# Three PE convolution tiles instead of six, stored weight parts in layer two, and a last stage in two parts per row

## The chip, the cores and the metric

One core of a Trainium2 chip runs the whole program. It has four compute engines, each with its own instruction stream taken strictly in order: PE (TensorE, matrix multiplies), DVE (VectorE), ACT (ScalarE) and POOL (GpSimd). A fifth stream, SP, issues every DMA of this kernel. The metric is device time in microseconds (us) for one execution. [...]

## The reference

A sequence of 2048 tokens of 1024 channels goes through two layers and a final RMSNorm. Layer one mixes a causal pooling and a state-space scan; the change leaves it alone. Layer two is the part that matters here:

```
h    = rmsnorm(x)
val, gt, z = split(h @ w_in, 3)                       # w_in: 1024 x 3072
g    = val * sigmoid(gt)
c    = depthwise_causal_conv(g, conv_w) + conv_b      # 31 taps for each of 1024 channels
c    = layernorm_over_channels(c) * ln_g + ln_b
x    = x + (silu(c) * silu(z)) @ w_out                # w_out: 1024 x 1024
out  = x * rsqrt(mean(x*x) + eps) * final_norm
```

All inputs and outputs are float32.

## The kernel before

**Halves and units.** The tokens are processed in two halves, A and B, of 1024. PE's work is a fixed list of units: layer one's projections of A and of B, its output of A, layer two's projections of A, layer one's output of B, layer two's projections of B, and then the last projection of A (`A.q`) and of B (`B.q`). A projection unit makes one tile of 128 channels by 1024 tokens with 48 matmuls of 128x512, since each product of float32 numbers is taken in three (high by high, high by low, low by high) of parts in fp32r. An output unit is 48 matmuls as well. Layer two of a half has 24 projection units: `g` and `v` for each channel tile j (gate and value), then eight `y` units (the second gate z).

**Weights.** A weight tile is loaded into `raw`; ACT rounds it into a high part (`w<-raw`, a CAST) and DVE subtracts for the low part. Four pairs of `w` slots exist; `fetch_thread` loads, `split_thread` splits. Half B loads and splits the same weights again.

**Convolution.** Each channel tile of a half is convolved by DVE or by PE. On DVE, ACT makes the first tap into an accumulator `ca`, and 30 SCALAR_TENSOR_TENSOR instructions add one tap each to the same accumulator. The last two tiles are done in two token blocks of 512. On PE (`pe_conv`) the tile goes through DRAM buffers `gpd`, a band of the taps is spread by ACT with a mask (24 instructions for each of two channel halves), and each channel half takes two chunks of 12 matmuls. `PEB = (6, 7)` are tiles that PE convolves for both halves at once; `PEC` adds 4 and 5 for half B alone. So PE convolves six of the sixteen half-tiles in four passes, and DVE the other ten.

**Layer norm and gates.** `ln_thread(h, b, ...)` normalises one block b of 512 tokens of half h, when all eight channel tiles of that half are stored in `cd`. It loads four tiles, sums them (DVE), gets the mean from PE, subtracts, squares (ACT), gets the variance from PE, takes a power on POOL, spreads it by PE, and multiplies. PE thus holds three small groups of matmuls for each of the four blocks, at fixed places of its stream. Half A's results go through DRAM (`y1d`) and are split by `y1_thread`; `A.q` needs block 0, then block 1. `B.q` needs those of half B.

**Last stage.** `evac1` takes a row tile of 128 tokens: the residual is loaded, the matmul's result added for each channel half eh, ACT sums the squares, and with the second half POOL makes the factor `rs` and DVE scales 1024 columns by `rs` and `final_norm` in one instruction; one DMA stores them.

**What sets the order.** All this is written as generators. When the program is built, a planner (`Sched`) steps them with estimated durations and emits, engine by engine, the instruction that can start first, ties broken by RANK; PE's unit list has the lowest rank and fills what is left. So the streams' order depends on the estimates, but is fixed in the program. `Alloc` takes slots of a pool (`ca` 2, `cg` 2, `w` 8); `free` gives them back.

Of the kernel before, what the change touches and what calls it, by code (L numbers as in the profile page):

```python
# [10 lines left out]
F32 = mybir.dt.float32  # L11
F32R = mybir.dt.float32r
# [25 lines left out]
PAD = {("PE", True): 5.0, ("PE", False): 0.3, ("V", True): 1.0, ("V", False): 0.05, ("A", True): 1.0, ("A", False): 0.05}  # L38
SLOTS = dict(act=25, w=8, raw=2, st=8, po=2)
NSSM = 3  # L40
RANK = dict(split=2, pool=4, pec=3, lna=8, lnb=3, y1=3, ssm=4, prep=2)
PEB = (6, 7)
PEC = (4, 5) + PEB
ORDER = (range(NK), (0, 1, 6, 7, 2, 3, 4, 5))


VECS = {"even_norm": 8, "odd_norm": 8, "pool_scale": 4, "ssm_d": 4, "conv_b": 8, "conv_ln_g": 8, "conv_ln_b": 8}
# [29 lines left out]
class Sched:  # L77
# [170 lines left out]
def trunk(ctx, tc, io):  # L248
# [13 lines left out]
    def slots(pool, n, width=1024, where=const):  # L262
        sc.pool(pool, n, lambda i, dt, name: where.tile([128, width], dt, tag=f"{pool}{i}", name=name))
# [4 lines left out]
    slots("st", SLOTS["st"], SLOT)  # L268
    slots("po", SLOTS["po"], SLOT)
    slots("cg", 2, SLOT)  # L270
    slots("ca", 2)
    slots("sml", 12, 16)
    slots("pwt", 1, 128)
    slots("sml2", 1, 64)
# [17 lines left out]
    def width(o):  # L292
        return int(np.prod(o.shape[1:]))
# [94 lines left out]
    def mmb(batch):  # L388

        d = 0.0  # L390
        for o, w, x, s, e in batch:
            if x.dtype == F32R:
                d += width(o) / 2216.0
            elif w.shape[1] > 64:
                d += max(0.224, width(o) * 1e-3)
            else:
                d += 0.07 + width(o) * 0.5e-3

        def emit():
            for o, w, x, s, e in batch:  # L400
                nc.tensor.matmul(o, w, x, start=s, stop=e)  # L401
        rd = []
        wr = []
        for o, w, x, s, e in batch:
            for l, ap in ((rd, w), (rd, x), (wr, o)):
                if not any(ap is y for y in l):
                    l.append(ap)
        op = Op("PE", d, rd, wr, emit)
        op.n = len(batch)
        return op  # L410
# [68 lines left out]
    class Job:  # L479
        def __init__(self, src, name, key=("go",)):  # L480
            self.src, self.name, self.pool, self.key = src, name, "w", key

        def release(self):
            free(self.pool, self.hi, self.lo)

    def job_cols(w, c0, name):
        return Job(w[c0 // 128], name)
# [10 lines left out]
    jobs = []  # L498
    jobs_parts = {}

    def fetch_thread(jobs):
        for job in jobs:
            job.raw = yield Alloc("raw")
            yield Wait(job.key)
            yield dma(job.raw, job.src)
            done("raw", job)

    def split_thread(jobs):
        for job in jobs:
# [918 lines left out]
    def conv_load():  # L1428
        for h, j in conv_order:
            yield Wait(("g", h, j))  # L1430
            gt = yield Alloc("cg")
            if h == 0:
                yield gset(gt[:, :HL], 0.0)
            else:
                yield dma(gt[:, :HL], gd[0][j][:, H - HL:H])
            yield dma(gt[:, HL:HL + H], gd[h][j])
            cgt[h, j] = gt
            yield Wait(("cw",))
            ca = cas[h, j] = yield Alloc("ca")
            yield act(ca[:, :H], gt[:, 0:H], AF.Identity, bias=vc("conv_b", j), scale=cwt[:, j, 0:1])  # L1440
            done("cg", h, j)

    cgt, cas = {}, {}

    def conv_thread():

        seq = [(h, j, (0, 1)) for h, j in conv_order[:-2]]
        seq += [(h, j, (b,)) for b in range(2) for h, j in conv_order[-2:]]
        for h, j, bl in seq:
            yield Wait(("cg", h, j))  # L1450
            gt, ca = cgt[h, j], cas[h, j]
            n0, n1 = bl[0] * 512, bl[-1] * 512 + 512
            acc = ca[:, n0:n1]
            for k in range(1, NT):
                yield stt(acc, gt[:, k + n0:k + n1], cwt[:, j, k:k + 1], acc, ALU.mult, ALU.add)
            if bl[-1] == 1:
                free("cg", gt)
            spawn(conv_store(h, j, ca, bl), 6, f"cs{h}{j}")

    def conv_store(h, j, ca, bl):  # L1460
# [124 lines left out]
    def ln_thread(h, b, out, gate=None):  # L1585
        if gate:
            yield Wait(gate)
        bs = slice(b * 512, (b + 1) * 512)
        for j in range(NK):
            yield Wait(("c", h, j, b))  # L1590
        if h == 0 or b == 0:
            ct = yield Alloc("act", 4)
            pools = ("act",) * 4
        else:
            pools = ("ca", "ca", "cg", "cg")
            ct = yield Alloc("ca", 2)
            ct += yield Alloc("cg", 2)
        cc = [c[:, :1024] for c in ct]
        for kp in range(4):
            yield dma(k2(cc[kp]), cd[h][kp][:, :, bs])  # L1600
        sm_, vs_, q_ = yield Alloc("st", 3)
        sm, vs, sq = sm_[:, :1024], vs_[:, :1024], q_[:, :1024]
        yield tt(sm, cc[0], cc[1], ALU.add)
        for c in cc[2:]:
            yield tt(sm, sm, c, ALU.add)
        yield tt(sm[:, 0:512], sm[:, 0:512], sm[:, 512:1024], ALU.add)
        mups = yield Alloc("aux")
        yield mmb([(mups, onesN, sm[:, 0:512], True, True)])
# [85 lines left out]
    def evac1(h):  # L1694
        tag = f"{P[h]}.q"

        def half(eh, tp, s, ps):
# [3 lines left out]
            if eh == 0:  # L1701
                yield dma(xt[:, 0:512], rowd[:, 0:512])
            else:
                yield dma(xt[:, 512:1024], rowd[:, 512:1024])
                yield Wait(("x2", h, t))
                yield dma(xt[:, 0:512], x2d[h][t])
            yield Wait(("pe", tag, eh, tp, s))
            xv = xt[:, eh * 512:(eh + 1) * 512]
            yield tt(xv, xv, ps[:, s * 512:(s + 1) * 512], ALU.add)
# [9 lines left out]
            yield tt(ms, ssq[h][:, t, 0:1], ssq[h][:, t, 1:2], ALU.add, G)  # L1719
            yield ts(ms, ms, 1.0 / D, RMS_EPS, ALU.mult, ALU.add, G)  # L1720
            yield from rsqrt_of(rs, ms, 1)
            yield Wait(("fnb", h))
            x = xt[:, :1024]
            yield stt(x, x, rs, fnb[0], ALU.mult, ALU.mult)
            free("sml", sm)
            r0 = h * H + t * 128
            yield dma(io["out"][0, r0:r0 + 128, :], x)
            free("st", xt)

        def f(eh, tp, ps):  # L1730
# [120 lines left out]
    spawn(after(("y1d", 0, 3), ln_thread(0, 1, None)), RANK["lna"], "lnA1")  # L1851
    spawn(y1_thread(0, y1[0], ("u", GATE_Y)), RANK["y1"], "y1A0")
    spawn(after((y1[0].name, 7, 0), y1_thread(1, y1[0], ("u", GATE_Y))), RANK["y1"], "y1A1")
    spawn(ln_thread(1, 0, y1[1]), RANK["lnb"], "lnB0")
    spawn(ln_thread(1, 1, y1[1]), RANK["lnb"], "lnB1")
    spawn(fnb_thread(0, ("u", "A.q.e0t3")), 4, "fnb")
    done("fnb", 1)
    sc.run()
# [42 lines left out]
```

## Time and profile before

| what | us |
|---|---|
| median of 3 runs (1501.55 to 1502.56) | 1502.55 |
| the profiled execution | 1500.32 |
| its span, first to last instruction | 1498.5 |
| PE busy | 1467.7 |
| DVE busy | 1104.4 |
| ACT busy | 524.7 |
| DMA queue's packets, share of 16 engines | 55.5% |

In the profile a row of the timeline gives start, duration, engine, line, operation, output<-inputs with buffer numbers left out, shape and count, and in brackets the idle time just ahead of it with what ended it. A row of the wait list says which line waited for which engine, the total, the number of times and the longest. Lines L319, L337, L351, L363 and L401 are the helpers that record a tensor_tensor, a scalar_tensor_tensor, an ACT copy, an ACT activation and a matmul, so groups are told apart by tile names.

In time, layer two of half A begins on PE at 576 us, layer one's output of B follows from 847 us, layer two of half B from 983 us, `A.q` from 1303 us and `B.q` from about 1398 us.

### The profile page before, as it was taken

How to read it: one execution, taken by the hardware profiler on the slowest of the kernel's cores; microseconds unless marked ns; L12 is line 12 of the kernel's file. 1: busy time of each engine (PE TensorE's matmuls, PEld its weight loads, DVE VectorE, ACT ScalarE, POOL GpSimd, SP SyncE). 2: the span in 40 equal slices, each digit the busy share in tenths (PEclk: the TensorE clock that was granted, in tenths of full speed). 3: DMA queues.
4: the chain of work that ended last, by engine and by line, in shares of the span. 5: the costliest groups of instructions: out<-in, count | busy, mean ns of one | idle time of the engine just before them, and what ended most of it. 6: DMA issues, size and time to landing. Idle time of an engine off the chain costs nothing. (4 is left out here: it accounts for less than half of the span.)

```text
span 1498.5 us, 17919 instructions
## 1 busy us (share of the span) xinstructions
PE 1467.7 (98%) x6768; PEld 1202.1 (80%) x6768; DVE 1104.4 (74%) x1333; ACT 524.7 (35%) x834; POOL 89.7 (6%) x297
## 2 busy tenths in 40 slices
PE   7999899999999999999999999999999999999997
PEld 5887688888888888888888888888888788887785
DVE  7988583997975224699999998247987998987632
ACT  6235341112143035211111521352364556544411
POOL 1000100000000011000000000110000000003321
PEclk9999999999999999999999999999999999999999
DMA  9579946556475462331343543524557475957752
GB/s 350 197 212 335 336 165 247 194 189 239 161 268 151 125 206 85 112 111 59 99 127 113 210 140 128 183 70 128 109 156 227 138 244 185 385 202 248 260 171 109
DMA packets 161159, 276.26 MB, mean 184 GB/s; under 512 B 53184, under 2 KB 83632, under 8 KB 161072
## 3 DMA queue, kind: packets, MB, share of 16 engines
q1 hardware_dynamic: 161072, 275.12, 55.5%
q8 instruction: 53, 0.87, 0.2%
q14 instruction: 34, 0.28, 0.1%
HBM read 181.56 MB, written 93.51 MB: 184 GB/s over the span
## 5 line engine op out<-in xcount | busy, mean ns | idle before, releaser
L401 PE MATMUL mm<-act,w 128*128 128x512 f32 x4224 | 1003.8, 397 | 9.6 <-ACT act L363 6.6
L401 PEld LDWEIGHTS mm<-act,w 128*128 128x128 f32 x4224 | 793.2, 189 | 190.5 <-ACT act L363 6.6
L337 DVE SCALAR_TENSOR_TENSOR ca<-cg,cwt,ca 128x1024 f32<-128x1024 f32 (+1 forms) x360 | 397.5, 1106 | 12.8 <-ACT ca L363 2.5
L401 PE MATMUL mm<-w,act 128*128 128x512 f32 x1344 | 315.9, 395 | 0.8 <-DVE w L319 0.8
L401 PEld LDWEIGHTS mm<-w,act 128*128 128x128 f32 x1344 | 251.7, 188 | 59.4 <-DVE w L319 1.1
L319 DVE TENSOR_TENSOR w<-raw,w 128x1024 fp32r<-128x1024 f32 (+1 forms) x119 | 141.9, 1195 | 106.8 <-ACT w L351 106.1
L351 ACT CAST w<-raw 128x1024 fp32r<-128x1024 f32 (+1 forms) x119 | 121.6, 1022 | 214.9 <-PE mm L401 141.6
L363 ACT ACTIVATE junk<-st 128x1024 bf16<-128x1024 f32 (+1 forms) x64 | 54.0, 844 | 123.8 <-DVE st L319 116.1
L319 DVE TENSOR_TENSOR st<-st,mm 128x512 f32<-128x512 f32 x48 | 30.9, 683 | 76.2 <-PE mm L401 76.2
L351 ACT CAST act<-st 128x512 fp32r<-128x512 f32 (+1 forms) x64 | 51.8, 855 | 57.2 <-DVE st L337 16.6
L363 ACT ACTIVATE po<-mm 128x1024 f32<-128x1024 f32 x28 | 28.7, 1025 | 112.4 <-PE mm L401 70.7
L319 DVE TENSOR_TENSOR act<-st,act 128x512 fp32r<-128x512 f32 (+1 forms) x64 | 56.4, 922 | 14.7 <-ACT act L351 14.6
L401 PE MATMUL aux<-st,act 128*128 128x128 f32 (+2 forms) x448 | 63.8, 289 | 0.0
L363 ACT ACTIVATE act<-act,mask 128x128 f32<-128x128 f32 x192 | 58.0, 392 | 16.5 <-DMA act<-band 16.5
L401 PEld LDWEIGHTS aux<-st,act 128*128 128x128 f32 x448 | 57.2, 191 | 2.9
L363 ACT ACTIVATE st<-mm 128x1024 f32<-128x1024 f32 x24 | 24.6, 1024 | 81.5 <-PE mm L401 81.5
L337 DVE SCALAR_TENSOR_TENSOR act<-aux,vcol,act 128x512 fp32r<-128x512 f32 x32 | 22.6, 746 | 41.0 <-ACT act L363 41.0
L317 POOL TENSOR_TENSOR sml<-sml,mhalf 128x1 f32<-128x1 f32 (+2 forms) x38 | 30.3, 798 | 336.8 <-DVE sml L327 335.2
L351 ACT COPY st<-aux 128x256 f32<-128x256 f32 (+3 forms) x50 | 21.4, 445 | 75.2 <-PE aux L401 56.9
L329 POOL TENSOR_SCALAR sml<-sml 128x1 f32<-128x1 f32 (+2 forms) x72 | 25.7, 357 | 365.3 <-ACT junk L363 360.6
L401 PE MATMUL mm<-act,act 128*128 128x512 f32 x192 | 45.0, 394 | 0.8 <-DVE st L319 0.8
L337 DVE SCALAR_TENSOR_TENSOR st<-st,mm 128x1024 f32<-128x1024 f32 x24 | 34.2, 1424 | 14.7 <-PE mm L401 8.8
(144 smaller groups left out, 873.0 us busy)
## 6 DMA issues: line engine op xcount, KB each, us to landing
raw<-in_odd_w_in SPq DMA_DIRECT2D x48, 512.0 KB, 3.9
st<-x1d SPq DMA_DIRECT2D x48, 256.0 KB, 4.9
raw<-in_even_w_in SPq DMA_DIRECT2D x23, 512.0 KB, 5.7
st<-in_xT SPq DMA_DIRECT2D x16, 512.0 KB, 5.9
st<-in_x SPq DMA_DIRECT2D x16, 512.0 KB, 7.9
raw<-in_even_w_out SPq DMA_DIRECT2D x16, 512.0 KB, 3.9
z1d<-po SPq DMA_DIRECT2D x16, 512.0 KB, 3.2
st<-z1d SPq DMA_DIRECT2D x16, 512.0 KB, 6.5
```

Source lines behind the costliest of these rows:

```text
L317: return Op("G", d, [a, b], [o], lambda: G.tensor_tensor(o, a, b, op))
L319: return Op("V", d, [a, b], [o], lambda: V.tensor_tensor(o, a, b, op))
L329: e.tensor_scalar(o, a, s1, s2, op0, op1)
L337: return Op("V", d, rd, [o], lambda: V.scalar_tensor_tensor(o, a, s, b, op0, op1))
L351: return Op("A", adur(o, a, 0), [a], [o], lambda: A.copy(o, a))
L363: return Op("A", adur(o, a, n), rd, wr, lambda: A.activation(o, a, fn, **kw))
L401: nc.tensor.matmul(o, w, x, start=s, stop=e)
```

## The change

The change has five parts. First, `PEB` becomes empty and `PEC` is `(5, 6, 7)`: PE convolves three tiles of half B alone, and DVE the other thirteen half-tiles; half B's tiles come in the order 0, 1, 2, 6, 3, 7, 4, 5. Second, a tile's convolution on DVE has two accumulators, taps alternating between them: ACT makes the first two taps, DVE adds 29, and one more instruction adds the two accumulators. The pool `ca` has four slots. Third, half A's split weights for layer two are stored to DRAM (`keep_thread`), and half B's 24 units load both parts instead of loading `raw` and splitting. Fourth, the last stage multiplies the first channel half by `final_norm` ahead of the matmul's wait, so that ACT can scale it by `rs` while DVE does the second half; each half is stored by a DMA of its own. What is multiplied ahead is the finished sum of the first channel half, which was stored in `x2d` and loaded again. Fifth, all layer norm blocks but one take their four tiles from `ca`, both blocks of half B wait for the splits of half A, and the planner's estimate for one kind of matmul is higher. The buffer reserved for descriptors is set to 1024.

```
-PEB = (6, 7)
-PEC = (4, 5) + PEB
-ORDER = (range(NK), (0, 1, 6, 7, 2, 3, 4, 5))
+KEEP = (("wt", "0", "1"), ("wv", "0", "1"), ("w1z", "0", "1"),)
+PEB = ()
+PEC = (5, 6, 7)
+ORDER = (range(NK), (0, 1, 2, 6, 3, 7, 4, 5))
-    slots("ca", 2)
+    slots("ca", 4)
...
-                d += max(0.224, width(o) * 1e-3)
+                d += max(0.224, width(o) * 1.68e-3)
...
+    def keep_thread(job):
+        for d, t in zip(job.kept, (job.hi, job.lo)):
+            yield dma(d, t.bitcast(F32))
+        job.release()
+        done("kept", job)
...
     def fetch_thread(jobs):
+        prev = None
         for job in jobs:
+            if job.like:
+                if prev and not prev.like:
+                    yield Wait(("w", prev))
+                prev = job
+                yield Wait(("kept", job.like))
+                job.hi, job.lo = yield Alloc(job.pool, 2, F32R)
+                for d, t in zip(job.like.kept, (job.hi, job.lo)):
+                    yield dma(t.bitcast(F32), d)
+                done("w", job)
+                continue
...
-            ca = cas[h, j] = yield Alloc("ca")
+            ca, cb = cas[h, j] = yield Alloc("ca", 2)
             yield act(ca[:, :H], gt[:, 0:H], AF.Identity, bias=vc("conv_b", j), scale=cwt[:, j, 0:1])
+            yield act(cb[:, :H], gt[:, 1:H + 1], AF.Copy, scale=cwt[:, j, 1:2])
...
-            acc = ca[:, n0:n1]
-            for k in range(1, NT):
-                yield stt(acc, gt[:, k + n0:k + n1], cwt[:, j, k:k + 1], acc, ALU.mult, ALU.add)
+            acc = ca[:, n0:n1], cb[:, n0:n1]
+            for k in range(2, NT):
+                yield stt(acc[k % 2], gt[:, k + n0:k + n1], cwt[:, j, k:k + 1], acc[k % 2], ALU.mult, ALU.add)
+            yield tt(acc[0], acc[0], acc[1], ALU.add)
...
-        if h == 0 or b == 0:
-            ct = yield Alloc("act", 4)
-            pools = ("act",) * 4
-        else:
-            pools = ("ca", "ca", "cg", "cg")
-            ct = yield Alloc("ca", 2)
-            ct += yield Alloc("cg", 2)
+        pool = "act" if h == 1 and b == 0 else "ca"
+        pools = (pool,) * 4
+        ct = yield Alloc(pool, 4)
...
+                yield Wait(("fnb", h))
+                yield tt(xt[:, 0:512], xt[:, 0:512], fnb[0][:, 0:512], ALU.mult)
...
-            x = xt[:, :1024]
-            yield stt(x, x, rs, fnb[0], ALU.mult, ALU.mult)
+            r0 = h * H + t * 128
+            yield act(xt[:, 0:512], xt[:, 0:512], AF.Copy, scale=rs)
+            yield dma(io["out"][0, r0:r0 + 128, 0:512], xt[:, 0:512])
+            yield stt(xv, xv, rs, fnb[0][:, 512:1024], ALU.mult, ALU.mult)
+            yield dma(io["out"][0, r0:r0 + 128, 512:1024], xv)
...
-    spawn(ln_thread(1, 0, y1[1]), RANK["lnb"], "lnB0")
-    spawn(ln_thread(1, 1, y1[1]), RANK["lnb"], "lnB1")
+    spawn(ln_thread(1, 0, y1[1], (y1[0].name, NK - 1, 1)), RANK["lnb"], "lnB0")
+    spawn(ln_thread(1, 1, y1[1], (y1[0].name, NK - 1, 1)), RANK["lnb"], "lnB1")
```

Three places of the order show what moves. The first is DVE's stream around the first layer norm block (half A, block 0), in layer two's projections of half B. Before, the block's sums (`st<-act,act` and on) stand between taps of half B's last two tiles and splits of its weights:

```order
L319 TENSOR_TENSOR w_965_8323<-raw_947_8123,w_964_8322 128x1024
L337 SCALAR_TENSOR_TENSOR ca_951_8150<-cg_948_8125,cwt,ca_951_8150 128x512 x13
L319 TENSOR_TENSOR w_978_8408<-raw_959_8243,w_977_8407 128x1024
L337 SCALAR_TENSOR_TENSOR ca_951_8150<-cg_948_8125,cwt,ca_951_8150 128x512 x2
L337 SCALAR_TENSOR_TENSOR ca_968_8364<-cg_967_8344,cwt,ca_968_8364 128x512
L319 TENSOR_TENSOR st_979_8414<-act_971_8384,act_972_8385 128x1024
```

Now the same sums follow directly on the last taps of half A, behind the normed inputs of half B (`act<-aux,vcol,act`) and the addition of the two accumulators:

```order
L338 SCALAR_TENSOR_TENSOR act_864_7467<-aux_867_7487,vcol,act_863_7466 128x512
L338 SCALAR_TENSOR_TENSOR ca_785_6782<-cg_784_6771,cwt,ca_785_6782 128x1024
L338 SCALAR_TENSOR_TENSOR act_869_7494<-aux_870_7500,vcol,act_868_7493 128x512
L338 SCALAR_TENSOR_TENSOR act_869_7494<-aux_871_7513,vcol,act_868_7493 128x512
L320 TENSOR_TENSOR ca_785_6782<-ca_785_6782,ca_786_6783 128x1024
L320 TENSOR_TENSOR st_876_7560<-ca_872_7540,ca_873_7541 128x1024
L320 TENSOR_TENSOR st_876_7560<-st_876_7560,ca_874_7542 128x1024
L338 SCALAR_TENSOR_TENSOR st_879_7569<-st_879_7569,mm_854_7407 128x1024
```

The block has moved from the late units of half B to the early ones, and its tiles now take the slots that the accumulators of half A leave. PE's mean matmul of this block moved with it: before, 678 of half B's 1152 projection matmuls stood ahead of it; now 138 do.

The second place is DVE's stream at the end of half B's convolution. Before, the last taps stand between splits of half A's layer norm results (`act<-st,act`), of weights, and the sums of half B's block 0 (`st<-act,act`):

```order
L319 TENSOR_TENSOR act_1114_9558<-st_1111_9537,act_1113_9557 128x1024
L337 SCALAR_TENSOR_TENSOR ca_968_8364<-cg_967_8344,cwt,ca_968_8364 128x512 x3
L319 TENSOR_TENSOR act_1117_9562<-st_1115_9559,act_1116_9561 128x1024
L337 SCALAR_TENSOR_TENSOR ca_968_8364<-cg_967_8344,cwt,ca_968_8364 128x512
L319 TENSOR_TENSOR w_1125_9605<-raw_1100_9467,w_1124_9604 128x1024
L319 TENSOR_TENSOR st_1128_9613<-act_1118_9580,act_1119_9581 128x1024
```

Now the last taps stand alone, and half A's block 1 begins behind them (`st_1034`), then the first split of the last projection's weights and of half A's results:

```order
L338 SCALAR_TENSOR_TENSOR ca_983_8655<-cg_981_8640,cwt,ca_983_8655 128x512
L338 SCALAR_TENSOR_TENSOR ca_982_8654<-cg_981_8640,cwt,ca_982_8654 128x512
L320 TENSOR_TENSOR ca_982_8654<-ca_982_8654,ca_983_8655 128x512
L320 TENSOR_TENSOR st_1034_9306<-ca_1030_9298,ca_1031_9299 128x1024
L320 TENSOR_TENSOR st_1034_9306<-st_1034_9306,ca_1032_9300 128x1024
L320 TENSOR_TENSOR st_1034_9306<-st_1034_9306,ca_1033_9301 128x1024
L320 TENSOR_TENSOR st_1034_9306<-st_1034_9306 128x512
L320 TENSOR_TENSOR w_1042_9348<-raw_1026_9243,w_1041_9347 128x1024
```

The splits of half B's weights are gone from this stretch, block 1 of half A has moved behind the whole convolution, and both blocks of half B have moved behind it.

The third place is the end of DVE's stream, the last row tiles of `B.q` (`mm` is PE's result, `sml` holds `rs`). Before:

```order
L337 SCALAR_TENSOR_TENSOR st_1273_10819<-st_1273_10819,sml_1278_10899,act_1152_9860 128x1024
L319 TENSOR_TENSOR st_1275_10879<-st_1275_10879,mm_1274_10878 128x512
L337 SCALAR_TENSOR_TENSOR st_1275_10879<-st_1275_10879,sml_1281_10949,act_1152_9860 128x1024
L319 TENSOR_TENSOR st_1276_10880<-st_1276_10880,mm_1274_10878 128x512
L337 SCALAR_TENSOR_TENSOR st_1276_10880<-st_1276_10880,sml_1283_10974,act_1152_9860 128x1024
```

And now:

```order
L320 TENSOR_TENSOR st_1244_10952<-st_1244_10952,mm_1243_10951 128x512
L338 SCALAR_TENSOR_TENSOR st_1242_10890<-st_1242_10890,sml_1247_10974,act_1116_9855 128x512
L338 SCALAR_TENSOR_TENSOR st_1244_10952<-st_1244_10952,sml_1250_11021,act_1116_9855 128x512
L320 TENSOR_TENSOR st_1245_10953<-st_1245_10953,mm_1243_10951 128x512
L338 SCALAR_TENSOR_TENSOR st_1245_10953<-st_1245_10953,sml_1252_11055,act_1116_9855 128x512
```

The scaling has half the columns, and the first addition of the last unit now stands ahead of the scaling of the row tile before it.

More of the change, by code (lines that the diff above doesn't have):

```diff
@@ L40 @@
 NSSM = 3
-RANK = dict(split=2, pool=4, pec=3, lna=8, lnb=3, y1=3, ssm=4, prep=2)
-PEB = (6, 7)
-PEC = (4, 5) + PEB
-ORDER = (range(NK), (0, 1, 6, 7, 2, 3, 4, 5))
+KEEP = (("wt", "0", "1"), ("wv", "0", "1"), ("w1z", "0", "1"),)
+RANK = dict(keep=5, split=2, pool=4, pec=3, lna=8, lnb=3, y1=3, ssm=4, prep=2)
+PEB = ()
+PEC = (5, 6, 7)
+ORDER = (range(NK), (0, 1, 2, 6, 3, 7, 4, 5))
 VECS = {"even_norm": 8, "odd_norm": 8, "pool_scale": 4, "ssm_d": 4, "conv_b": 8, "conv_ln_g": 8, "conv_ln_b": 8}
@@ L481, in __init__ @@
             self.src, self.name, self.pool, self.key = src, name, "w", key
+            self.kept = self.like = None
+            self.refs = 1
         def release(self):
-            free(self.pool, self.hi, self.lo)
+            self.refs -= 1
+            if self.refs == 0:
+                free(self.pool, self.hi, self.lo)
     def job_cols(w, c0, name):
@@ L499, in trunk, with keep @@
     jobs_parts = {}
+    def keep(pairs):
+        for n, (a, b) in enumerate(pairs):
+            a.kept = [dram(f"kept{len(keeps)}_{p}", (128, 1024)) for p in "hl"]
+            a.refs = 2
+            b.like = a
+            keeps.append(a)
+    keeps = []
+    def keep_thread(job):
[3 more added lines that the diff above has]
+        done("kept", job)
     def fetch_thread(jobs):
+        prev = None
         for job in jobs:
+            if job.like:
[8 more added lines that the diff above has]
+                continue
+            prev = job
             job.raw = yield Alloc("raw")
@@ L509, in split_thread @@
         for job in jobs:
+            if job.like:
+                continue
             job.hi, job.lo = yield Alloc(job.pool, 2, F32R)
@@ L522, in split_thread @@
             done("w", job)
+            if job.kept:
+                spawn(keep_thread(job), RANK["keep"], "keep")
     class Acts:
@@ L1450, in conv_thread @@
             yield Wait(("cg", h, j))
-            gt, ca = cgt[h, j], cas[h, j]
+            gt, (ca, cb) = cgt[h, j], cas[h, j]
             n0, n1 = bl[0] * 512, bl[-1] * 512 + 512
-            acc = ca[:, n0:n1]
-            for k in range(1, NT):
-                yield stt(acc, gt[:, k + n0:k + n1], cwt[:, j, k:k + 1], acc, ALU.mult, ALU.add)
+            acc = ca[:, n0:n1], cb[:, n0:n1]
+            for k in range(2, NT):
+                yield stt(acc[k % 2], gt[:, k + n0:k + n1], cwt[:, j, k:k + 1], acc[k % 2], ALU.mult, ALU.add)
+            yield tt(acc[0], acc[0], acc[1], ALU.add)
             if bl[-1] == 1:
                 free("cg", gt)
+                free("ca", cb)
             spawn(conv_store(h, j, ca, bl), 6, f"cs{h}{j}")
@@ L1721, in half @@
             yield from rsqrt_of(rs, ms, 1)
-            yield Wait(("fnb", h))
-            x = xt[:, :1024]
-            yield stt(x, x, rs, fnb[0], ALU.mult, ALU.mult)
+            r0 = h * H + t * 128
[3 more added lines that the diff above has]
+            yield dma(io["out"][0, r0:r0 + 128, 512:1024], xv)
             free("sml", sm)
-            r0 = h * H + t * 128
-            yield dma(io["out"][0, r0:r0 + 128, :], x)
             free("st", xt)
@@ L1779, in trunk @@
     out_units(1, "B.q", io["odd_w_out"], y1[1], evac1(1), True)
+    named = {j.name: j for j in jobs}
+    pairs = []
+    for j in jobs:
+        for pre, a, b in KEEP:
+            if j.name.startswith(pre + a):
+                pairs.append((j, named[pre + b + j.name[len(pre + a):]]))
+    keep(pairs)
     def main():
@@ L1888 @@
     from concourse.bass_utils import run_bass_kernel_spmd
-    nc = bacc.Bacc("TRN2", target_bir_lowering=False, num_devices=1)
+    nc = bacc.Bacc("TRN2", target_bir_lowering=False, num_devices=1, dynamic_dma_scratch_size=1024)
     arrays, io = {}, {}
```

## The prediction

> **What bounds the kernel now.** I read the engine totals first, then PE's rows with a wait in brackets, then the rows of each stage.
>
> ```profile
> span 1498.5 us, 17919 instructions
> PE 1467.7 (98%) x6768; PEld 1202.1 (80%) x6768; DVE 1104.4 (74%) x1333; ACT 524.7 (35%) x834; POOL 89.7 (6%) x297
> ```
>
> PE is busy 98% of the span. The other engines matter only where PE waits for them. From layer two on those waits are these, each the bracket at a row's end:
>
> ```profile
> 1165.35 1.10 PE L401 MATMUL aux<-st,onesN 128*128 128x512 f32 x2 [0.45 <-DVE st L319]
> 1178.00 1.05 PE L401 MATMUL aux<-onesN,st 128*128 128x1 f32 x8 [0.42 <-DVE st L319]
> 1372.21 1.13 PE L401 MATMUL aux<-st,ones 128*128 128x128 f32 x8 [1.16 <-DVE st L327]
> 1405.08 15.30 PE L401 MATMUL mm<-w,act 128*128 128x512 f32 x65 [0.76 <-DVE w L319]
> 1485.67 3.76 PE L401 MATMUL mm<-act,act 128*128 128x512 f32 x15 [0.78 <-DVE st L319]
> ```
>
> Together 3.57 us, three of them at the layer norm blocks. So the time is the sum of PE's work; a change gains by taking matmuls off PE, by shortening what follows PE's end, and loses by new waits.
>
> One matmul's price comes from two long runs without a wait:
>
> ```profile
> 819.78 70.94 PE L401 MATMUL mm<-act,w 128*128 128x512 f32 x306
> 890.56 74.91 PE L401 MATMUL mm<-w,act 128*128 128x512 f32 x324
> 982.71 7.79 PE L401 MATMUL mm<-act,w 128*128 128x512 f32 x33
> ```
>
> (890.56 - 819.78) / 306 = 0.2313 us start to start, so a unit of 48 is 11.10 us. Half B's 24 units of layer two begin at 982.71.
>
> **PE convolutions, the main term.** Sixteen chunks (four passes of four) become twelve. A chunk is 12 matmuls for two token blocks:
>
> ```profile
> 1100.09 2.87 PE L401 MATMUL aux<-st,act 128*128 128x128 f32 x24
> 1102.71 1.62 PE L401 MATMUL mm<-act,w 128*128 128x512 f32 x6
> 1104.17 5.52 PE L401 MATMUL aux<-st,act 128*128 128x128 f32 x48
> 1109.45 1.63 PE L401 MATMUL mm<-act,w 128*128 128x512 f32 x6
> 1110.91 2.84 PE L401 MATMUL aux<-st,act 128*128 128x128 f32 x24
> 1113.51 16.95 PE L401 MATMUL mm<-act,w 128*128 128x512 f32 x72
> 1224.10 2.79 PE L401 MATMUL aux<-st,act 128*128 128x64 f32 x24
> ...
> 1237.51 5.83 PE L401 MATMUL mm<-act,w 128*128 128x512 f32 x24
> ```
>
> From 1100.09 to 1113.51 stand four chunks and 12 projection matmuls: (13.42 - 12 x 0.2313) / 4 = 2.66 us. The other shape, 1224.10 to 1237.51 with the same contents, gives 2.66 too. Four chunks fewer: **-10.7 us**, all of it on the bound engine.
>
> **DVE, which takes over three half-tiles.** It pays only if DVE keeps up. A tap on the same accumulator against an operation that doesn't use the previous result:
>
> ```profile
> 882.33 1.22 DVE L319 TENSOR_TENSOR w<-raw,w 128x1024 fp32r<-128x1024 f32 x1
> 883.46 1.29 DVE L319 TENSOR_TENSOR act<-st,act 128x512 fp32r<-128x512 f32 x2
> 884.67 6.56 DVE L337 SCALAR_TENSOR_TENSOR ca<-cg,cwt,ca 128x1024 f32<-128x1024 f32 x5
> 891.14 1.21 DVE L337 SCALAR_TENSOR_TENSOR st<-st,mm 128x1024 f32<-128x1024 f32 x1
> L337 DVE SCALAR_TENSOR_TENSOR ca<-cg,cwt,ca 128x1024 f32<-128x1024 f32 x240 | 307.6, 1284 | 9.3 <-ACT ca L363 2.3
> L337 DVE SCALAR_TENSOR_TENSOR ca<-cg,cwt,ca 128x512 f32<-128x512 f32 x120 | 89.8, 751 | 3.5 <-ACT ca L363 0.2
> ```
>
> Five chained taps span 6.56 us and one lasts 1.284, so they start (6.56 - 1.284) / 4 = 1.319 us apart. The fifth starts at 889.95, and the next, independent instruction at 891.14, only 1.19 later. A split gives the same sign: the next starts 883.46 - 882.33 = 1.13 later. I take 1.19 for alternating taps: a tile is 29 x 1.19 + 1.13 = 35.6 us, against 30 x 1.319 = 39.6. Half-width taps I take at 0.751 - (1.284 - 1.19) = 0.66, as much below their own duration. No row shows alternating taps themselves; the bounds are 1.13 and 1.319.
>
> [...]
>
> Now the schedule, in the new order. The stretches lie between DVE instructions that PE or the preceding stage ties to a time:
>
> ```profile
> 624.86 1.22 DVE L337 SCALAR_TENSOR_TENSOR st<-st,mm 128x1024 f32<-128x1024 f32 x1 [0.35 <-PE mm L401]
> 858.37 1.21 DVE L337 SCALAR_TENSOR_TENSOR st<-st,mm 128x1024 f32<-128x1024 f32 x1
> 901.79 1.22 DVE L319 TENSOR_TENSOR po<-po,mm 128x1024 f32<-128x1024 f32 x1 [0.68 <-PE mm L401]
> 992.09 1.41 DVE L337 SCALAR_TENSOR_TENSOR act<-aux,vcol,act 128x512 fp32r<-128x512 f32 x2 [3.92 <-ACT act L363]
> 1000.99 1.41 DVE L337 SCALAR_TENSOR_TENSOR act<-aux,vcol,act 128x512 fp32r<-128x512 f32 x2 [1.55 <-ACT act L363]
> ```
>
> - 624.86 to 858.37 (233.5 us): 152 taps x 1.19 = 180.9, 21 splits x 1.13 = 23.7, gate products and sums about 19.8. Sum 224: 9 us in hand.
> - 901.79 to 992.09 (90.3 us): 56 taps = 66.6, the rest 21. Sum 88: 2.5 us in hand.
> - Half A's last tile is added up at about 1003.4, just behind 1000.99. Block 0 of half A has moved forward, so a store and a load stand between, then two sums of 1.9 together.
>
> ```profile
> cd<-ca SPq DMA_DIRECT2D x8, 512.0 KB, 5.2
> act<-cd SPq DMA_DIRECT2D x12, 512.0 KB, 5.9
> raw<-in_odd_w_in SPq DMA_DIRECT2D x48, 512.0 KB, 3.9
> ```
>
> 1003.4 + 0.8 (the addition) + 5.2 + 5.9 + 1.9 = 1017.2. PE has 138 projection matmuls and the state-space remainder of layer one's output (about 3.4 us) ahead of its mean matmul: 982.71 + 138 x 0.2313 + 3.4 = 1018.0. So the block arrives **with about 1 us in hand**. From mean to variance PE has 48 matmuls, as before, where they took 1178.00 - 1165.35 = 12.65 us with a wait of 0.42.
>
> The block ends on DVE near 1046. Half B's convolution and what is mixed in (87 full taps, 116 of half width at 0.66, which is 180; gates and splits 15) add up to 195 us: 1243 with the small waits of its gates. Store, load and sums make 1256. PE reaches block 1's mean at 982.71 + 1020 x 0.2313 + 12 x 2.66 + 3.4 + 2.3 (other small matmuls) = 1256.2. Again even, within 3 us. The blocks of half B follow behind with one or two us in hand at best.
>
> Four blocks that each arrive within a few us of PE: I take 6.6 us of waits instead of 3.6, **+3.0 us**. Bounds: -3.6 (today's waits go as well) and +12 (3 us more at each block).
>
> **Kept weights.** They take 24 splits from DVE's units of half B (24 x 1.13 = 27 us, in the 195 already) and 24 casts from ACT, and give SP 48 stores and 48 loads of 512 KB for 24 loads. SP waits on slots now for long stretches:
>
> ```profile
> SPq L386 <- DVE w L319: 320.8, 92, 23.3
> ```
>
> Four pairs of `w` slots last four units, 44 us; a pair of loads, two times 3.9, fits in that. I count it at nothing, covered by the three other pairs. Without that cover it is late loads: the whole 7.8 us, once per unit at worst, which is rival three. ACT's 13 more first taps and 16 scaled halves fall on an engine busy 35%: nothing.
>
> **The tail.** What follows PE's last matmul:
>
> ```profile
> 1488.73 1.28 DVE L337 SCALAR_TENSOR_TENSOR st<-st,sml,act 128x1024 f32<-128x1024 f32 x1 [3.11 <-POOL sml L317]
> 1489.93 0.68 DVE L319 TENSOR_TENSOR st<-st,mm 128x512 f32<-128x512 f32 x1
> 1493.72 1.28 DVE L337 SCALAR_TENSOR_TENSOR st<-st,sml,act 128x1024 f32<-128x1024 f32 x1 [3.11 <-POOL sml L317]
> out<-st SPq DMA_DIRECT2D x16, 512.0 KB, 2.8
> x2d<-st SPq DMA_DIRECT2D x16, 256.0 KB, 2.2
> ```
>
> The last scaling halves from 1.28 to about 0.7 (-0.5), its DMA from 2.8 to 2.2 less 0.3 for a second issue (-0.3), and the addition no longer stands behind a 1.28 us scaling (-0.3). **-1.1 us**, bounds -0.4 and -1.5.
>
> **Sum.** Profiled execution 1500.32 (span 1498.5 and 1.8 around it): 1500.32 - 10.7 - 1.1 + 3.0 = 1491.5. The median of the runs is 1502.55, 2.2 above that execution, so 1493.7. From the bounds -3.6 to +12 in place of +3.0, the terms reach from 1487 to 1503; their ends are unlikely together, and this case's own range is 1489 to 1498.5.
>
> **Rivals.**
> - *Layer norm waits eat the gain.* Half A's block 0 and block 1 stand even with PE, each behind a store and load of 11 us that nothing overlaps, and DVE has no spare work ahead of them. With 2.5 us more at every block, 10 in all, the time is 1500 to 1505. Against it: PE's positions leave room between later steps of a block (72 matmuls from mean to variance for block 1, 126 for the last).
> - *Alternation doesn't shorten the spacing* (the slower side). With taps at 1.319, 208 taps of half A cost 26.8 us more against 9 + 2.5 in hand: 15 us late at block 0. Half B's taps, 87 x 0.129 and 116 x 0.1 (as an estimate), are 23 us late at block 1. Nothing lies between to catch up, since the convolution itself feeds PE's block: 1493.7 - 3 + 15 + 22 = 1528. It decides above 1.25 us a tap (11.5 us / 208 = 0.055 more than 1.19). Against it stands the 1.19 behind the chained taps. [...]
> - *Kept loads come late.* SP is one queue in order; a store of a kept part waits for its split, and everything behind waits as well. At 1 us a unit it is +24: 1518. Against it: the loads are short, and four slots of cover.
> - *The tile count doesn't bring what it says*, if the removed chunks filled PE's waits. They would then be worth less than 10.7; but PE's rows around them have no waits, so I give this nothing of its own.
>
> **How the numbers follow.** The forecast has 0.76, layer norm waits 0.11, alternation 0.06, kept loads 0.05, and 0.02 for the rest. The range 1488.5 to 1500 holds the forecast and the lower end of the first rival, and leaves out the others. Within 0.2% is 1499.5 to 1505.6, about what a measurement can tell from no change: that is the first rival, 0.10. Slower is the two others, 0.11. Faster is the forecast and what is left of the first rival and the rest, 0.79.
>
> **What would show it.** PE's chunk rows: 12 groups, no passes in half A. DVE's alternating taps 1.17 to 1.22 us apart in half A; 1.25 or more means the second rival. PE's rows at the four layer norm blocks: waits of 0 to 2 us each, block 0 of half A near 1018, block 1 near 1256. `A.q` starts near 1292. No wait of PE for a DMA of `w`. From PE's end to the span's end 8 us instead of 9. I am wrong if a single layer norm row shows a wait over 4 us, or PE waits for weights in half B.

## The result, and the profile after

Before 1502.55 us (median), after **1523.4 us**: ratio 1.0134, 95% interval 1.0107 to 1.0161. It is 1.3% slower, where 1493.7 and a range of 1488.5 to 1500 were predicted. The profiled execution took 1525.8 us, 2.4 above the median and 25.5 more than the one of before.

The page of the changed kernel, span and busy times of the engines:

```profile
span 1523.9 us, 17909 instructions
PE 1469.5 (96%) x6672; PEld 1196.4 (79%) x6672; DVE 1157.7 (76%) x1415; ACT 507.1 (33%) x788; POOL 104.2 (7%) x296
```

PE is still the bound. It has 96 matmuls fewer and yet is as long busy, since some of them ran longer. POOL was busy 89.7 us before; it has one instruction fewer now and 14.5 us more. The waits tell where. PE's timeline of the changed kernel, from layer one's last output on (start, duration, shape, count, idle time ahead and what ended it):

```profile
898.48 74.79 PE L402 MATMUL mm<-w,act 128*128 128x512 f32 x324
976.61 0.33 PE L416 MATMUL aux<-ident,st 128*128 128x128 f32 x1 [3.12 <-ACT st L364]
978.33 4.44 PE L402 MATMUL mm<-w,act 128*128 128x512 f32 x12
983.39 3.04 PE L402 MATMUL mm<-w,act 128*128 128x512 f32 x12
996.31 8.51 PE L402 MATMUL mm<-act,w 128*128 128x512 f32 x36
1011.25 0.47 PE L416 MATMUL aux<-ident,st 128*128 128x128 f32 x1 [6.21 <-ACT st L364]
1023.21 17.50 PE L402 MATMUL mm<-act,w 128*128 128x512 f32 x75
1280.14 1.10 PE L402 MATMUL aux<-st,onesN 128*128 128x512 f32 x2 [0.81 <-DVE st L320]
1313.43 27.79 PE L402 MATMUL mm<-w,act 128*128 128x512 f32 x120
1344.37 2.08 PE L402 MATMUL aux<-st,onesN 128*128 128x512 f32 x2 [3.15 <-DVE st L320]
1345.46 12.40 PE L402 MATMUL mm<-w,act 128*128 128x512 f32 x42
1392.15 1.05 PE L402 MATMUL aux<-onesN,st 128*128 128x1 f32 x8 [2.46 <-DVE st L320]
1431.03 0.51 PE L402 MATMUL mm<-w,act 128*128 128x512 f32 x1 [2.66 <-ACT w L352]
1510.42 5.15 PE L402 MATMUL mm<-act,act 128*128 128x512 f32 x21 [0.78 <-DVE st L320]
```

The kernel before has these rows at the same places:

```profile
576.32 7.79 PE L401 MATMUL mm<-act,w 128*128 128x512 f32 x33
1000.43 9.90 PE L401 MATMUL mm<-act,w 128*128 128x512 f32 x42
1302.53 9.89 PE L401 MATMUL mm<-w,act 128*128 128x512 f32 x42
```

The stretches between the same marks, before (left) and after:

| stretch of PE | before, us | after, us | difference |
|---|---|---|---|
| start to layer two of A | 576.3 | 583.8 | +7.5 |
| layer two of A and the projections of B's output | 314.2 | 314.6 | +0.4 |
| B's output, norm of B's rows (to 1000.43 / 1023.21) | 109.9 | 124.7 | **+14.9** |
| rest of layer two of B, to `A.q` | 302.1 | 290.2 | **-11.9** |
| `A.q` and `B.q`, to PE's end (1489.43 / 1515.57) | 186.9 | 202.1 | **+15.2** |
| PE's end to the span's end | 9.1 | 8.3 | -0.7 |

So the gain from PE's convolution came, and three losses stand against it: layer one, the norm of half B's rows, and the last stage. (Three projection matmuls, 0.7 us, stand on the other side of the mark at 1000.43 / 1023.21 now, so the norm's loss is 14.2 us and the gain 11.2.) A second thing shows in the rows: behind two of these waits PE was slow for a while. Behind the wait of 3.12 us the 12 matmuls at 978.33 took 4.44 us at a granted clock of 0.66 (978 to 983 us), the 12 at 983.39 only 3.04 at 1.00 (983 to 987 us). The granted clock was 0.91 from 975 to 1012 us, and 1.00 in that stretch before; it was 0.78 from 1344 to 1358 us, behind the wait of 3.15 us.

### The profile page after: what moved, and what is told of

Its sections match the earlier page's. It is cut to its first block, busy times and chain, and to the rows that moved or that the text cites. A ratio compares the mean times of both kernels' runs of the same rounds, so it can differ in the third digit from the quotient of the medians.

```text
span 1523.9 us, 17909 instructions
## 1 busy us (share of the span) xinstructions
PE 1469.5 (96%) x6672; PEld 1196.4 (79%) x6672; DVE 1157.7 (76%) x1415; ACT 507.1 (33%) x788; POOL 104.2 (7%) x296
## 4 chain that ended last, share of the span: by engine, by line
PE 68%; DVE 13%; DMA 8%; POOL 4%; issue 3%; SPq 2%; ACT 2%; DVEq 0%; ACTq 0%; POOLq 0%
PE mm L402 64%; DVE st L320 4%; DVE ca L338 4%; PE aux L402 3%; POOL sml L318 3%; SPq L387 2%; POOL sml L330 1%; DVE act L320 1%; DVE st L348 1%; DMA raw<-in_even_w_in 1%; DVE w L320 1%; DMA ca<-cd 1%; DMA y1d<-st 1%; PE aux L416 1%; DMA st<-x2d 1%
## 5 line engine op out<-in xcount | busy, mean ns | idle before, releaser
L402 PE MATMUL mm<-act,w 128*128 128x512 f32 x4224 | 1005.0, 397 | 10.6 <-ACT act L364 7.0
L338 DVE SCALAR_TENSOR_TENSOR ca<-cg,cwt,ca 128x1024 f32<-128x1024 f32 (+1 forms) x435 | 463.4, 1137 | 3.8 <-ACT ca L364 3.8
L402 PE MATMUL mm<-w,act 128*128 128x512 f32 x1344 | 322.9, 401 | 4.9 <-ACT w L352 3.2
L402 PEld LDWEIGHTS mm<-w,act 128*128 128x128 f32 x1344 | 256.4, 192 | 66.0 <-ACT w L352 4.1
L320 DVE TENSOR_TENSOR w<-raw,w 128x1024 fp32r<-128x1024 f32 (+1 forms) x95 | 112.4, 1187 | 85.9 <-ACT w L352 83.6
L352 ACT CAST w<-raw 128x1024 fp32r<-128x1024 f32 (+1 forms) x95 | 96.6, 1017 | 138.3 <-PE mm L402 103.9
L318 POOL TENSOR_TENSOR sml<-sml,mhalf 128x1 f32<-128x1 f32 (+2 forms) x38 | 34.0, 894 | 350.1 <-DVE sml L328 348.5
L402 PE MATMUL aux<-st,act 128*128 128x64 f32 (+1 forms) x352 | 53.0, 293 | 1.4 <-DVE st L320 1.2
L402 PEld LDWEIGHTS aux<-st,act 128*128 128x128 f32 x352 | 45.6, 191 | 6.0 <-DVE st L320 3.5
L364 ACT ACTIVATE st<-st,sml 128x1024 f32<-128x1024 f32 (+1 forms) x32 | 29.1, 934 | 56.2 <-POOL sml L318 54.7
L364 ACT ACTIVATE act<-act,mask 128x128 f32<-128x128 f32 x144 | 43.3, 391 | 8.3 <-DMA act<-band 8.3
```

The source lines that it names most:

```text
L318: return Op("G", d, [a, b], [o], lambda: G.tensor_tensor(o, a, b, op))
L320: return Op("V", d, [a, b], [o], lambda: V.tensor_tensor(o, a, b, op))
L338: return Op("V", d, rd, [o], lambda: V.scalar_tensor_tensor(o, a, s, b, op0, op1))
L352: return Op("A", adur(o, a, 0), [a], [o], lambda: A.copy(o, a))
L364: return Op("A", adur(o, a, n), rd, wr, lambda: A.activation(o, a, fn, **kw))
```

## The experiments

Each edit is shown against the changed kernel, or against the base where that is named. Ratios are to the kernel before on the same chip (medians of 1501.7 to 1503.7 us). Experiments 9 to 12 ran on another chip than the base that they are set against, so there times are compared by their ratios.

**1. Norm factors on VectorE.** In the changed kernel taps run in the stretch in which DVE stood idle before (7.54 and 9.75 us, as a row shows below), ACT's scaling of the rows waits for POOL's factor, and PE's waits there are 3.12 + 0.71 + 6.21 + 0.57 = 10.6 us. DVE's taps, POOL's small instructions for one pair of rows and ACT's scaling, in the changed kernel:

```profile
1001.00 8.46 DVE L338 SCALAR_TENSOR_TENSOR ca<-cg,cwt,ca 128x1024 f32<-128x1024 f32 x7
1001.76 0.57 POOL L330 TENSOR_SCALAR sml<-sml 128x1 f32<-128x1 f32 x1 [8.73 <-ACT junk L364]
1002.41 1.46 POOL L318 TENSOR_TENSOR sml<-sml,mhalf 128x1 f32<-128x1 f32 x1
...
1006.00 2.31 POOL L330 TENSOR_SCALAR sml<-sml 128x1 f32<-128x1 f32 x2
1008.27 1.58 POOL L318 TENSOR_TENSOR sml<-sml,mhalf 128x1 f32<-128x1 f32 x1
1009.83 0.18 POOL L318 TENSOR_TENSOR sml<-sml,sml 128x1 f32<-128x1 f32 x1
1010.05 2.19 ACT L364 ACTIVATE st<-st,sml 128x1024 f32<-128x1024 f32 x2 [7.20 <-POOL sml L318]
```

The same chain for half A of the same kernel, where no tap runs (first and last row), and the kernel before at half B (DVE's idle time, ACT's wait):

```profile
549.19 0.19 POOL L330 TENSOR_SCALAR sml<-sml 128x1 f32<-128x1 f32 x1 [58.38 <-ACT junk L364]
...
552.55 0.19 POOL L318 TENSOR_TENSOR sml<-sml,sml 128x1 f32<-128x1 f32 x1
```

```profile
946.11 1.28 DVE L319 TENSOR_TENSOR st<-st,mm 128x512 f32<-128x512 f32 x2 [7.54 <-PE mm L401]
957.14 1.29 DVE L319 TENSOR_TENSOR st<-st,mm 128x512 f32<-128x512 f32 x2 [9.75 <-PE mm L401]
950.66 2.19 ACT L363 ACTIVATE st<-st,sml 128x1024 f32<-128x1024 f32 x2 [1.50 <-POOL sml L317]
```

A TENSOR_SCALAR on one column takes 0.19 us alone and 0.57 to 1.12 beside these taps; the chain of twelve instructions for a pair of rows takes 3.6 us alone and 9.2 beside them (549.19 to 552.74, 1001.76 to 1010.98). As soon as the run of taps ends, at 1009.46, the last instructions take 0.18 again. In the same kernel POOL's instructions took 0.19 beside two kinds of DVE's that read one input from PSUM: at 965.15 and 965.43 beside `st<-st,mm` (965.01 to 966.29), and at 988.27 and 988.54 beside `act<-aux,vcol,act` (987.72 to 989.12). Both tiles that a tap reads, `cg` and `ca`, are in SBUF. The kernel before already shows the effect on a single instruction: the power (the TENSOR_TENSOR with `mhalf`) takes 0.54 us at 985.47 and 1.52 at 987.05, where DVE runs a split from 986.94 on. Do PE's 10.6 us come from POOL's late factors, or from taps that stand on DVE ahead of the norm's own instructions? The test moves all but the power to DVE (`rsqrt_of` gets the engine as an argument, not shown):

```
-        yield ts(ms, ss, 1.0 / D, RMS_EPS, ALU.mult, ALU.add, G)
-        yield from rsqrt_of(rs, ms, 1)
+        yield ts(ms, ss, 1.0 / D, RMS_EPS, ALU.mult, ALU.add, V)
+        yield from rsqrt_of(rs, ms, 1, V)    # the power still on G
```

> The changed kernel with the row scaling of layer one's output norm on VectorE but for the power, which stays on GpSimd. [...]

Measured: **1507.2 us**, ratio to the kernel before 1.0019 (1.0005 to 1.0033). PE's only wait in the stretch, and ACT's for the factor:

```profile
997.00 0.77 PE L416 MATMUL aux<-ident,st 128*128 128x128 f32 x5 [0.46 <-ACT st L364]
956.09 2.19 ACT L364 ACTIVATE st<-st,sml 128x1024 f32<-128x1024 f32 x2 [1.88 <-DVE sml L320]
```

10.6 us of waits became 0.46, with as much work on the accumulators in the stretch from 937.5 to 1012.5 us (47.5 us of DVE's time, 48.1 in the changed kernel, none before); the time fell by 16. The profiled execution gains it in this place: from the first matmul of layer one's output of B to `A.q` it takes 399.1 us instead of 415.0, and from there to PE's end 200.5 instead of 202.1. So these waits came from POOL's late factors: they went when the factors left POOL, with the taps still there.

**2. One accumulator.** Are the taps to blame because they follow without a gap, or any taps?

```
-            acc = ca[:, n0:n1], cb[:, n0:n1]
-            for k in range(2, NT):
-                yield stt(acc[k % 2], ..., acc[k % 2], ...)
-            yield tt(acc[0], acc[0], acc[1], ALU.add)
+            acc = ca[:, n0:n1]
+            for k in range(1, NT):
+                yield stt(acc, ..., acc, ...)
...
```

The second accumulator's slot and its first tap on ACT go as well.

> The changed kernel with one accumulator per tile, each tap on the result of the one before. Theory P1 (only taps without a gap keep GpSimd out): half B's norm chains are 3.5 to 5 us a pair and PE's waits there fall below 3 us, but VectorE is late at the layer norm blocks, 1535 to 1545. Theory P2 (any tap with two SBUF inputs keeps GpSimd out): the chains stay 8 to 10 us, the waits near 10, and with VectorE late by 15 and 22 us the time is 1550 to 1562. Theory A (alternation gained nothing on VectorE): within 3 us of 1523.4.

Measured: **1558.6 us** (1.0367, 1.0338 to 1.0396). DVE's taps and ACT's wait at the same place:

```profile
998.95 9.08 DVE L338 SCALAR_TENSOR_TENSOR ca<-cg,cwt,ca 128x1024 f32<-128x1024 f32 x7
1008.11 2.19 ACT L364 ACTIVATE st<-st,sml 128x1024 f32<-128x1024 f32 x2 [7.31 <-POOL sml L318]
```

Taps are (9.08 - 1.28) / 6 = 1.30 us apart, and POOL is as late as with alternating taps: two TENSOR_SCALAR instructions took 2.56 us at 1004.20, and 2.31 at 1006.00 in the changed kernel. So it is any taps (P2). What brought them there is the division of the convolution: with the former one (experiment 8) DVE spends no time on accumulators from 937.5 to 1012.5 us (half A's last store from `ca` is issued at 908.46, half B's first load of `cg` at 1018.56). The kernel is 35 us slower than the changed one, but not by the spacing alone. Half A's block 0 now stands behind the whole convolution (its mean at 1292.68 us, at 1040.55 in the changed kernel), and `A.q` waits 17.45 and 15.30 us for half A's results:

```profile
1292.68 1.02 PE L402 MATMUL aux<-st,onesN 128*128 128x512 f32 x2
1328.76 11.51 PE L402 MATMUL mm<-w,act 128*128 128x512 f32 x36 [17.45 <-ACT act L352]
```

How much of the 35 us is the spacing and how much the moved block wasn't separated.

**3. The planner's former estimate.**

```
-                d += max(0.224, width(o) * 1.68e-3)
+                d += max(0.224, width(o) * 1e-3)
```

> The changed kernel with the planner's former estimate of 1e-3 us per column for that matmul. Theory E (the estimate moved layer one's state-space matmuls ahead of their inputs): PE's waits of 0.3 to 0.7 us between 262 and 412 us, 2.4 us together, go, and PE starts layer two about 2 to 4 us earlier; the time falls to 1519 to 1521. Rival (they are the runs' own spread): layer two starts within 1 us of 583.8 and the time is within 2 us of 1523.4.

Measured: **1514.2 us** (1.0068, 1.0048 to 1.0088), more than either theory gave. A state-space matmul of the start and layer two's first matmul, in the kernel before, the changed one and this one:

```profile
169.28 0.27 PE L415 MATMUL aux<-ident,sml 128*8 128x128 f32 x1 [3.21 <-POOL sml L317]
```

```profile
171.28 0.27 PE L416 MATMUL aux<-ident,sml 128*8 128x128 f32 x1 [3.47 <-POOL sml L318]
583.84 7.79 PE L402 MATMUL mm<-act,w 128*128 128x512 f32 x33
```

```profile
168.88 0.27 PE L416 MATMUL aux<-ident,sml 128*8 128x128 f32 x1 [2.84 <-POOL sml L318]
575.95 7.79 PE L402 MATMUL mm<-act,w 128*128 128x512 f32 x33
```

From the first to the second it is 407.0, 412.6 and 407.1 us: the estimate costs 5.5 us in layer one, which the change was said to leave alone. Of these 2.4 us are short waits for DVE, of which the longest is

```profile
360.91 1.10 PE L402 MATMUL aux<-act,st 128*128 128x256 f32 x4 [0.73 <-DVE st L320]
```

and the other two kernels have none; the other 3.1 us are longer rows of the same 1791 instructions. The state-space matmul near 170 us starts between 167.6 and 172.6 us over all kernels, and at 167.6 and 171.6 in the base and in the kernel without the hold (experiments 5 and 6), which differ only behind layer one; so I take what lies ahead of it for the runs' own spread. Of the 12.6 us between the two profiled executions 2.4 are this start, 5.5 layer one and 3.0 the last stage, where the order differs too (202.1 and 199.2 us).

**4. The former last stage**: `evac1` as before the change, one scaling on DVE and one DMA a row tile.

> The changed kernel with the former last stage: one scaling of 1024 columns on VectorE and one DMA for a row tile. Theory S (SP stands at stores of the first halves, which wait for GpSimd's factor, and the last weights' loads stand behind them): the four waits for w near 1424 to 1432 us (0.57 + 0.94 + 2.66 + 0.76 = 4.9 us) fall below 1.5, and the time falls by 3 to 7 us less the 1 us that the tail loses, to 1517 to 1521. Rival (the weights are late because half B's layer norm is): these waits stay and the time is 1523 to 1526.

Measured: **1529.5 us** (1.0168, 1.0139 to 1.0198). The waits for `w` didn't go; one grew to 6.11 us. Theory S falls, and the new last stage is worth about 6 us: in the profiled executions 4.4 from `A.q` to PE's end (206.5 us instead of 202.1) and 1.4 behind it (9.7 instead of 8.3). What makes the waits for `w` wasn't found.

**5 to 8. The base, and what makes the last stage long.** The base has repairs 1 and 3. In the others one thing is changed on it: no hold on half B's blocks (`ln_thread(1, b, y1[1])` without the gate); `PEC = (4, 5, 6, 7)`; `PEB`, `PEC` and `ORDER` of the kernel before.

> The changed kernel with both repairs: layer one's norm factors on VectorE but for the power, and the planner's former estimate. If the two losses are separate, 5.5 us (planner, between the start and layer two) go off the 1507.2 us of the first repair alone: 1500 to 1503. From A.q's first matmul to PE's last, 199 to 202 us as before the repairs (186.9 in the kernel before).

> The same base without the waits that hold half B's layer norm blocks until half A's results are split. Theory G (that hold makes these blocks late): the stretch from A.q's first matmul to PE's last shrinks by 6 us or more from its 199 to 202, and the time to 1492 to 1496. Theory D (VectorE comes to the blocks late, because it convolves three more half-tiles first) and theory S (loads behind stores on SP): the stretch stays within 3 us and so does the time.

> The same base with four PE tiles for half B (4, 5, 6, 7): 16 chunks as in the kernel before, VectorE has 12 half-tiles. Theory D: PE works 10.7 us more, and the stretch from A.q to PE's end shrinks by 8 to 13 us, so the time is within 3 us of the base. Theories G and S: the stretch stays at 199 to 202 and the time is 10 to 11 us above the base, near 1512.

> The same base with the kernel before's division of the convolution (four passes on PE, ten half-tiles on VectorE) and its tile order. Theory D: the stretch from A.q to PE's end is 187 to 191 us, and with 10.7 us more of PE's work the time is 1498 to 1504. Theories G and S: the stretch stays at 199 to 202 us and the time is 1510 to 1514.

| kernel | us | ratio to before, interval | `A.q` to PE's end, us |
|---|---|---|---|
| base | 1500.6 | 0.9991 (0.9974 to 1.0007) | 200.8 |
| no hold | 1517.3 | 1.0112 (1.0095 to 1.0129) | 214.5 |
| four PE tiles | 1505.9 | 1.0024 (1.0002 to 1.0046) | 193.4 |
| former split | 1518.6 | 1.0119 (1.0103 to 1.0134) | 204.9 |

The repairs add. Theory G falls: the hold helps, since without it `A.q` waits 6.91 and 7.27 us for half A's results. Theory D holds in part for four PE tiles (the stretch shrinks by 7.4, short of 8 to 13, and the time is 5.3 above the base's, not within 3) and not at all for the former split, and this miss shows the cause. SP's queue with the former split, the last store from PE's passes, the last from DVE's accumulators, and the first loads of a layer norm block:

```profile
1166.29 0.38 SPq L387 DMA_DIRECT2D cd<-st  x1
...
1222.12 0.32 SPq L387 DMA_DIRECT2D cd<-ca  x1
1222.49 1.86 SPq L387 DMA_DIRECT2D ca<-cd  x3
```

and DVE in the changed kernel, half B's last addition and block 1 of half A behind it:

```profile
1266.30 0.69 DVE L320 TENSOR_TENSOR ca<-ca,ca 128x512 f32<-128x512 f32 x1
1275.38 1.23 DVE L320 TENSOR_TENSOR st<-ca,ca 128x1024 f32<-128x1024 f32 x1 [8.39 <-DMA ca<-cd]
```

In both the layer norm block begins only behind the convolution's last store. With the former split even half A's block 0 does, whose inputs were all stored by 1166 us, 56 us earlier. The block takes four tiles from `ca`, `ca` has four, and a running tile holds two.

**9. Blocks in act again** (on the base; `act` is a pool of 25 tiles):

```
-        pool = "act" if h == 1 and b == 0 else "ca"
+        pool = "act" if h == 0 or b == 0 else "ca"
```

> The base (both repairs) with half A's layer norm blocks taking their four tiles from act again instead of the four accumulators. Theory Q (a block that needs all four accumulators can't start while any convolution runs, so block 1 of half A comes behind the whole convolution of half B and pushes both blocks of half B into the last stage): block 1's mean moves from 1273 to before 1110 us, the stretch from A.q's first matmul to PE's last falls from 200.8 to 187 to 192 us, and the time from 1500.6 to 1488 to 1494. Rival R (the last stage is slow for its own reasons): the stretch stays within 4 us of 200.8 and the time within 4 of 1500.6.

Measured: **1493.1 us**, ratio to the kernel before **0.994 (0.9919 to 0.9962)**: faster than both. Block 1's mean of half A, `A.q`'s first matmul, the mean of half B's first block and the last row, in this kernel:

```profile
1076.37 1.12 PE L402 MATMUL aux<-st,onesN 128*128 128x512 f32 x2 [0.43 <-DVE st L320]
1291.35 15.44 PE L402 MATMUL mm<-w,act 128*128 128x512 f32 x66
1306.62 1.12 PE L402 MATMUL aux<-st,onesN 128*128 128x512 f32 x2
1476.65 5.12 PE L402 MATMUL mm<-act,act 128*128 128x512 f32 x21 [0.78 <-DVE st L320]
```

and in the base:

```profile
1273.43 1.02 PE L402 MATMUL aux<-st,onesN 128*128 128x512 f32 x2
1289.08 4.35 PE L402 MATMUL mm<-w,act 128*128 128x512 f32 x18
1332.72 1.13 PE L402 MATMUL aux<-st,onesN 128*128 128x512 f32 x2
1484.80 5.11 PE L402 MATMUL mm<-act,act 128*128 128x512 f32 x21 [0.78 <-DVE st L320]
```

Block 1 stands 197 us earlier, half B's first block 15 us behind `A.q`'s start instead of 44, and the stretch is 190.4 us instead of 200.8. Theory Q holds. The waits for `w` are smaller but not gone (2.65 us in five rows, 4.0 in three in the base).

**10 and 11. All factors on VectorE**, on the base and with the blocks in act.

> The base with all factors of the layer norm blocks and of the last stage on VectorE too, but for the power. Theory R (GpSimd's chains, slowed by VectorE, hold ScalarE's scalings and with them the casts of the last weights behind them): PE's waits for w between 1390 and 1402 us (0.68 + 2.71 + 0.64 = 4.0) fall below 1.5 and the time falls by 3 to 7 us, to 1494 to 1498. Theory Q: the waits of the layer norm blocks stay and the time is within 3 us of 1500.6.

> Both edits on the base, the blocks in act and all factors on VectorE. If Q and R each hold and add: stretch 184 to 190 us, time 1484 to 1490. If only Q: as the blocks in act alone, within 2 us.

Measured: **1507.5 us** (1.0024, 1.0013 to 1.0036) and **1491.9 us** (0.9928, 0.9913 to 0.9943). Alone it was a miss: the waits for `w` went, and one of 8.65 us for half B's split results took their place. With the blocks in act it can't be told from act alone.

**12. No stored weights**: `KEEP = ()` on the base.

> The base without stored weight parts: half B loads and splits its weights again, 24 splits of 1.13 us more on VectorE (27 us) and 25 MB fewer stores. Theory D (VectorE is the limit in half B's convolution): block 1's mean comes 15 to 27 us later with a wait on PE, the time is 1512 to 1528. Theory K (the stored parts' DMAs delay the last stage): the time is 1495 to 1499. If neither, within 3 us of 1500.6.

Measured: **1533.2 us** (1.0197, 1.018 to 1.0214), beyond theory D's 1528. The order differs here as well: both blocks of half A come behind the convolution, and PE waits 13.03 and 15.98 us for their results. By the ratios the stored parts are worth 31 us in this arrangement; how much of that is DVE's 27 us and how much the moved blocks wasn't separated.

## Why the prediction was wrong

- **PE's convolution, -10.7: right.** The rest of layer two of B is 11.9 us shorter, 0.7 of which is three matmuls that now stand ahead of the mark: 11.2. A chunk is what it was: two chunks and six matmuls from 1123.60 to 1130.28, (6.68 - 6 x 0.2313) / 2 = 2.65.

```profile
1123.60 2.79 PE L402 MATMUL aux<-st,act 128*128 128x64 f32 x24
1126.20 1.65 PE L402 MATMUL mm<-act,w 128*128 128x512 f32 x6
1127.68 2.79 PE L402 MATMUL aux<-st,act 128*128 128x64 f32 x24
1130.28 9.96 PE L402 MATMUL mm<-act,w 128*128 128x512 f32 x42
```

- **Alternating taps at 1.19: right.** (8.46 - 1.28) / 6 = 1.197 us, against 1.30 in experiment 2. One row behind the chained taps was enough to read it, and the rival that denied it fell.
- **The stretch from 901.79 to 992.09, "2.5 us in hand": the step that failed first.** DVE's own sum held: block 0 of half A didn't wait, and half B's last addition came within 2 us of the forecast once 22.4 us of later start are taken off. But the sum asked only whether DVE gets through its work, not what stood beside it: the idle DVE of that stretch let POOL finish its factors in 3.6 us. The taps made them 9.2, ACT and PE stood behind, and it cost 14.2 us with the slow clock, 0.91 from 975 to 1012 us (124.7 - 0.7 - 109.9, the 0.7 being the three matmuls). POOL, 6% busy, appears nowhere in the prediction's sum. The profile before had it: the power at 987.05, beside a split on DVE, took 1.52 us, and 0.54 at 985.47.
- **"+3.0 for four blocks": mis-sized, for lack of a step.** The sums were made for half A's two blocks, and both came as forecast (no wait at block 0, 0.81 us at block 1). For half B's blocks there stood only "one or two us in hand at best". That a block needs all four accumulators, and so half A's block 1 must follow the whole convolution, was in the order that was shown, and was read as a place and not as a tie. The last stage became 15.2 us longer: waits of 3.15 and 2.46 at the blocks and of 0.57, 0.94, 2.66 and 0.76 for `w`, and the slow clock behind them (0.78 from 1344 to 1358 us, 0.90 from 1393 to 1410). On the base, taking the tie out shortens that stretch by 10.4 us; the rest, the waits for `w` among it, stays open.
- **The planner's estimate had no term.** It moved layer one's matmuls: 5.5 us. The other 2 of the 7.5 us ahead of layer two are the start, which differs as much between kernels that are alike there.
- **Kept loads at nothing: right.** No unit of half B's layer two waits for `w`. ACT has 16 first taps more (26 for 10), not 13 as counted there.
- **The tail, -1.1:** 0.7 was measured against the kernel before, and 1.4 against the same kernel with the former last stage (experiment 4), where the stretch ahead of PE's end is worth 4.4 more.
- Of the rivals, the first named the layer norm blocks, but for half A's store and load, and half A's blocks came as forecast; its 1500 to 1505 us is about 20 too low. None had POOL.

With the three causes taken out (experiment 9) the kernel takes 1493.1 us, close to the 1493.7 that the prediction's terms gave. The terms come one by one as well: against the kernel before, the profiled execution is 10.9 us shorter from layer one's output of B to `A.q` (401.0, 412.0) and 0.7 at the tail, and 3.5 longer from `A.q` to PE's end, where +3.0 of waits were put.

## What to carry to other kernels

When work is moved into a stretch where an engine stood idle, ask which other engine lived off that idleness: here a chain of twelve one-column instructions on POOL went from 3.6 to 9.2 us because DVE began to work beside it. Count the slots that a block of work needs at once against those that a loop holds: a block that needs the whole pool can't overlap the loop, whatever the engines could do. And price every edit, a number in a planner's table too: it moved work in a part of the program that the change did not mean to touch.

## What was not expected of the hardware

- A one-column POOL instruction other than the power took 0.19 us alone and 0.46 to 1.28 us beside DVE's taps. The power took 0.54 to 0.56 alone and 1.46 to 1.59 beside them, but for one in experiment 2 (0.54 at 1006.72). This holds with taps that start 1.20 us apart, before the tap ahead has ended (1.28), and with those of experiment 2, 1.30 apart: a gap of 0.02 us between taps made POOL no faster.
- Behind the wait of 3.15 us PE ran slow for a while: 42 matmuls at 1345.46 took 12.40 us at a granted clock of 0.82 (1345.46 to 1358 us), 42 at 1130.28 took 9.96 at 1.00 (1130.28 to 1140 us). The two waits at half B's blocks, 3.15 and 2.46 us, cost about 3.1 and 1.7 us more in the rows behind them, an estimate from their lengths at 0.2313 us a matmul.
